# Loads of a residual input issued ahead, and LayerNorm sums with the data as the moving operand

## The chip, the cores and the metric

The kernel runs on one core of a Trainium2 chip. A core has a matrix engine (TensorE, PE in the profile, with its weight loads PEld), a vector engine (VectorE, DVE), an activation engine (ScalarE, ACT), a programmable vector engine (GpSimd, POOL) and an engine that here only issues transfers (SyncE, SP). Each engine works off its own instructions in order and waits on semaphores for the others. PE reads its operands from SBUF, 128 partitions wide, and writes to PSUM. In a matmul the stationary operand is loaded first and the moving operand then streams through it. POOL and SP each have a queue of DMA transfers. The metric is the device time of one execution in microseconds.

## What is computed

One layer of a hybrid decoder on 256 prompt tokens and 8 x 4 sample tokens (N = 288), model width 2048:

```python
mod = silu(c) @ w_ada + b_ada
sh1, sc1, g1, sh2, sc2, g2 = split(mod, 6)
u = layernorm(x) * (1 + sc1) + sh1
p = u @ w_in                       # gated short convolution | mLSTM heads | output gate o
...
mix = concat(y_conv, y_mlstm) @ w_out
x = layernorm(ALPHA * x + (1 + g1) * mix) * ln1_g + ln1_b
u2 = layernorm(x) * (1 + sc2) + sh2
a, g = split(u2 @ w_up, 2)
y = (silu(causal_dwconv3(a)) * g) @ w_down
x = layernorm(ALPHA * x + (1 + g2) * y) * ln2_g + ln2_b
```

All values are float32; the states of convolution and mLSTM are further outputs. The change lies at the first residual: the loading of `x` for `ALPHA * x`, and the sums over the 2048 features that the two layer norms behind it need.

## The kernel before

Activations lie with features on the partitions and tokens along the free dimension: a tile is 128 features x 288 tokens, and x is 16 tiles. Weights come in 128 x 128 blocks, 16 to a transfer of 1 MB (`raw`), in the order of a list `items` that `plan()` makes; SP issues the transfers as far as seven buffers allow. Each half of a transfer is split into a high part (`whi`, ACT, L314) and a low part (`wlo`, DVE, L327), two halves ahead of use, and each block is multiplied three times (`mm3`, L474 to L476). Other items of the list hold 1 MB of `w_ada` (kind `"a"`); `take()` runs such an item on PE at once (L381: eight instructions `adaps`), and `next_block()` takes those that stand ahead of the next weight block.

Stages around the change, in the program's order: the columns of the convolution (`hc`, `cg`, `bg`), the eight columns of the output gate (`o`), the 16 tiles of the output projection (`mix`, loop over m), then the first up columns (`up`).

Ahead of the o columns stands the loop that loads x again on POOL's queue, 144 KB a tile, into `xa` and scales it on POOL by ALPHA (L1081, L1082). Each mix tile m ends in `residual(xa[m], ...)` (L1234 to L1238, DVE: `xa += g1 * mix`, the 32 sample tokens apart). Behind tile 0 the side work `first_stats` has PE average tile 0 over its features (L1302), ACT copies the result out as `shift` (L1304), POOL subtracts it from `xa[1]` and `xa[2]` (L1306) and, called by `stats(m)`, from each further tile (L1296), and DVE from `xa[0]` (L1308). `stats(m)` then takes, per tile, three weighted accumulations (L1266, L1268) and three plain ones (L1275, L1278) on DVE, two squares on ACT (L1282, L1283). The last tile is not accumulated.

In the last mix tile and behind it, `sums` (L1368) has PE add over the features. The six columns are the mean z, three weighted sums w, x, b, the square q and the weighted square p. The data block of 128 tokens is the stationary operand and a column of 1/2048 the moving one, so that tokens come out on the partitions: three matmuls a sum, which PE runs as six instructions. The last tile's four linear sums come from one matmul with `w4` (four columns). From the result `S` a chain of small DVE and ACT instructions (L1423 to L1455, on 128 x 3 values in `sv`) makes both norms' scales; `tokens` (L1460) turns them back to feature layout (`rr`, copied to `R`, and `tokp`, copied to `tok`). `corr` (L1500) and `u2t` (L1493 to L1504) then make the operand of the up columns.

The last adaLN unit (g2, 16 items) is taken in parts: `G2_EARLY` items stand in the list ahead of the first up column (one is taken by `take()` among the sums, `G2_FIRST` ahead of `rr`, what is left behind `u2_hi(0)`), the others are mixed into the up columns.

Of the kernel before, what the change touches and what calls it, by code (L numbers as in the profile page):

```python
# [7 lines left out]
F32 = mybir.dt.float32  # L8
F32R = mybir.dt.float32r
AF = mybir.ActivationFunctionType  # L10
ALU = mybir.AluOpType

P = 128
# [4 lines left out]
N = NP + NS  # L18
# [15 lines left out]
LATE = 15  # L34
KOUT = 6
PREHI = 3
G2_FIRST = 2
CF_AT = 6
SUMS_AT = 11
UP_AT = 12  # L40
# [1 line left out]
STORES = [(0,), (1, 2), (3, 4, 5), (6, 7, 8), (9, 10, 11), (12, 13, 14), (15,)]  # L42
RES0 = 8
RES1 = 12
G2_EARLY = 5
MIX_LAST = 8
C_FIRST = 2
C_LAST = 3
# [165 lines left out]
def body(tc, d, off, items, blocks):  # L214
    nc = tc.nc
    V, A, G, T = nc.vector, nc.scalar, nc.gpsimd, nc.tensor
    from contextlib import ExitStack
    ctx = ExitStack()
    with ctx:
        pers = ctx.enter_context(tc.tile_pool(name="pers", bufs=1))  # L220
# [15 lines left out]
        def st(name, dt=F32):  # L236
            return slab.tile([P, N], dt, tag="t", name=nm(name))

        def mps(name, n=512):
            return misc.tile([P, n], F32, tag="m", name=nm(name))  # L240
# [20 lines left out]
        for i, a in enumerate(range(0, KB, 3)):  # L261
            b = min(a + 3, KB)
# [4 lines left out]
        pos = [0, 0]  # L267
# [9 lines left out]
        c = 0  # L277
# [84 lines left out]
        ones = pers.tile([P, P], F32, name="ones")  # L362
        badd = pers.tile([P, 6, KB], F32, name="badd")
        ident = sm("ident")
# [71 lines left out]
        def take():  # L436

            i = pos[0]
            it = items[i]
            load()  # L440
            r = raws.pop(i)
            pos[0] += 1
            if it[0] == "a":
                ada_item(it, r)
                free()
            else:
                c_item(it[1], r)
# [109 lines left out]
        for k in range(0, KB, 2):  # L557
            t = st("xsum")
# [9 lines left out]
        for k in range(KB):  # L568
            x, q = st("xc"), st("sq")
# [35 lines left out]
        S = {}  # L605
# [15 lines left out]
        stat = pers.tile([P, 6], F32, name="stat")  # L621
# [456 lines left out]
        xa = []  # L1078
        for m in range(KB):
            t = st("xa")  # L1080
            nc.gpsimd.dma_start(out=t, in_=xd[:, m])  # L1081
            G.tensor_scalar(t, t, ALPHA, None, ALU.mult)  # L1082
            xa.append(t)
        gb = pers.tile([P, 8, KB], F32, name="gb")
        bb1, gg, gbb, ngg2, gbb2, gs, ng = (gb[:, i] for i in range(7))
        w4 = pers.tile([P, 4], F32, name="w4")
        L = KB - 1
        tmp3 = pers.tile([P, 3, 8], F32, name="gbt3")
        cst = pers.tile([P, 6], F32, name="cst")
# [2 lines left out]
        def constants_1():  # L1092
            ps = mps("gbm", 2)
            T.matmul(ps, ones, tmp[:, :, 0], start=True, stop=True)
            yield 2
            V.tensor_copy(gbm, ps)

            yield 6
            V.tensor_scalar(bb1, b1v, gbm[:, 1:2], None, ALU.subtract)
            V.tensor_tensor(gg, g1v, g1v, ALU.mult)  # L1100
            V.tensor_tensor(gbb, g1v, bb1, ALU.mult)
            V.tensor_scalar(ngg2, gg, -2.0, None, ALU.mult)
            V.tensor_scalar(gbb2, gbb, 2.0, None, ALU.mult)
            V.tensor_scalar(ng, g1v, -1.0, None, ALU.mult)
            V.tensor_copy(w4[:, 0:1], ones[:, 0:1])
            for i, v in enumerate((g1v, ngg2, gbb2)):
                V.tensor_scalar(w4[:, i + 1:i + 2], v[:, L:L + 1], ones[:, 0:1], None, ALU.mult)
            V.tensor_tensor(gb[:, 7], bb1, bb1, ALU.mult)
            for j, v in enumerate((gg, gbb2, gb[:, 7])):
                V.tensor_tensor(tmp3[:, j, 0:8], v[:, 0:8], v[:, 8:16], ALU.add)  # L1110
                for n in (4, 2, 1):
                    V.tensor_tensor(tmp3[:, j, 0:n], tmp3[:, j, 0:n], tmp3[:, j, n:2 * n], ALU.add)
            yield 10
            ps = mps("gbm3", 3)
            T.matmul(ps, ones, tmp3[:, :, 0], start=True, stop=True)
            yield 2
            V.tensor_copy(cst[:, 0:3], ps)
            V.tensor_scalar(cst[:, 3:4], gbm[:, 0:1], -1.0, None, ALU.mult)
            V.tensor_scalar(cst[:, 4:5], cst[:, 1:2], -1.0, None, ALU.mult)
            V.tensor_scalar(cst[:, 5:6], cst[:, 2:3], EPS, None, ALU.add)  # L1120
# [125 lines left out]
        BLK = ((0, P), (P, 2 * P), (N - P, N))  # L1246
# [110 lines left out]
        stp = {}  # L1357

        def sums(name, x, c, stop=False):

            bank = c // 5
            start = bank not in stp
            if start:
                stp[bank] = mps("stat", 24)
            w = 4 if name == "lin" else 1
            rhs = w4 if name == "lin" else ones[:, 0:1]
            for i, (a, b) in enumerate(BLK):
                T.matmul(stp[bank][:, 8 * i + c:8 * i + c + w], x[:, a:b], rhs, start=start and i == 0,  # L1368
                         stop=stop and i == 2)

        def late_sums():
            yield SUMS_AT
# [38 lines left out]
        q, p = squares(KB - 1)  # L1411
        sums("z", acc1["z"], 0)
        sums("q", acc1["q"], 4)
        take()
        sums("lin", xa[KB - 1], 0)
        sums("q", q, 4, True)
        sums("p", p, 5, True)
        S, S5 = (stp[i].rearrange("p (b c) -> p b c", c=8) for i in range(2))
        c = [sv[:, :, i] for i in range(16)]
        mean, wp, wv, xv, bv, var1, t1, t2, r1, v2, r2, Rr = c[0:12]  # L1420
        MW = sv[:, :, 0:2]
# [10 lines left out]
        V.tensor_tensor(xv, xv, mean, ALU.mult)  # L1432
        for _ in s1:
            pass
        V.tensor_tensor(xv, xv, S5[:, :, 5], ALU.add)
        V.tensor_tensor(t1, wp, wp, ALU.mult)
        V.tensor_tensor(xv, xv, t1, ALU.subtract)
        V.tensor_tensor(xv, xv, r1, ALU.mult)
# [23 lines left out]
        def spread(j):  # L1462
            return lambda i: sv[:, i, j:j + 1].to_broadcast([P, P])

        for _ in range(G2_FIRST):
            if items[pos[0]][0] == "a":
                take()
        rps = mps("rr", N)
        tokens(rps, spread(11), P)
        R = st("R")  # L1470
# [69 lines left out]
        for j in (8, 12):  # L1540
            ps = mps("rb", N)
            tokens(ps, spread(j), P)
            t = st("rb")
# [237 lines left out]
```

## Time and profile before

| | us |
|---|---|
| median of 3 runs | 1559.61 |
| lowest and highest run | 1556.93, 1560.07 |
| profiled execution | 1565.79 |
| its span, first to last instruction | 1564.0 |
| PE busy | 1515.3 |
| DVE, ACT, POOL busy | 948.0, 588.4, 251.9 |

The mean granted clock of the profiled execution is 0.984. The profile is of one execution; its rows name engine, source line, operation and `out<-in` tiles, with start and duration in us, and in brackets the idle time of the engine before it and what ended it. A row of the table by stretches of time gives busy us of PE, PEld, DVE, ACT and POOL, the granted TensorE clock as a share of full speed, the DMA engines' share and GB/s. A float32 matmul of the program appears as two PE instructions. A PE that is called busy isn't always streaming: the profile counts an instruction's time whatever its size.

### The profile page before, as it was taken

The numbers are of one execution on the slowest core, as the hardware profiler recorded it, in microseconds if no ns is written. First come the engines' busy times: TensorE is split into PE (matmuls) and PEld (weight loads), VectorE is DVE, ScalarE is ACT, GpSimd is POOL, SyncE is SP. The second block draws the span as 40 slices with busy tenths as digits, with TensorE's granted clock in tenths as the row PEclk, the third lists the DMA queues.
The fourth block names the chain that finished last, engine by engine and source line by source line (L and its number), as shares of the span: only waits on it lengthen the run. The fifth ranks groups of instructions, "written<-read, shape, count | busy, mean of one in ns | idle before, by whom it ended". The sixth has DMA issues, their size and how long they took to land.

```text
span 1564.0 us, 28234 instructions
## 1 busy us (share of the span) xinstructions
PE 1515.3 (97%) x11762; PEld 1418.0 (91%) x11762; DVE 948.0 (61%) x1746; ACT 588.4 (38%) x880; POOL 251.9 (16%) x472
## 2 busy tenths in 40 slices
PE   9999999999999969999999999999999999999994
PEld 7988988888888859979999999999999999999994
DVE  6466566777865388677655545555555545555557
ACT  5533243422233224444433333344443334444334
POOL 3310005210112320003740000000000000000245
PEclk9999999999999979889999999999999999999997
DMA  9897778668898845364755644444444444444401
GB/s 387 342 346 297 285 301 324 236 225 341 326 372 316 299 173 208 135 243 145 259 204 228 222 162 165 161 170 173 168 166 166 162 164 170 173 167 165 162 28 61
DMA packets 49663, 343.90 MB, mean 220 GB/s; under 512 B 5888, under 2 KB 6400, under 8 KB 9088
## 3 DMA queue, kind: packets, MB, share of 16 engines
q1 hardware_dynamic: 46656, 329.09, 56.8%
q0 software_dynamic: 2736, 12.82, 2.1%
q8 instruction: 92, 1.51, 0.4%
q14 instruction: 35, 0.29, 0.1%
q10 hardware_dynamic: 144, 0.19, 0.0%
HBM read 329.77 MB, written 12.31 MB: 219 GB/s over the span
## 4 chain that ended last, share of the span: by engine, by line
PE 85%; DVE 5%; DMA 3%; issue 3%; POOL 2%; ACT 1%; SPq 0%; POOLq 0%; DVEq 0%; ACTq 0%
PE g L474 6%; PE g L476 5%; PE a L474 5%; PE g L475 5%; PE dn L476 5%; PE dn L474 5%; PE dn L475 5%; PE a L476 5%; PE a L475 5%; PE adaps L381 5%; PE h L474 5%; PE h L475 4%; PE h L476 4%; DMA xa<-xT 2%; PE mix L474 2%
## 5 line engine op out<-in xcount | busy, mean ns | idle before, releaser
L314 ACT CAST whi<-raw 128x1024 fp32r<-128x1024 f32 x410 | 424.1, 1046 | 402.8 <-PE dn L476 156.6
L327 DVE TENSOR_TENSOR wlo<-raw,whi 128x1024 fp32r<-128x1024 f32 x410 | 502.3, 1240 | 55.4 <-ACT whi L314 54.6
L476 PE MATMUL dn<-y2h,whi 128*128 128x288 f32 x704 | 208.0, 295 | 0.0
L474 PE MATMUL dn<-y2l,whi 128*128 128x288 f32 x704 | 207.7, 295 | 0.0
L475 PE MATMUL dn<-y2h,wlo 128*128 128x288 f32 x704 | 207.5, 295 | 0.0
L475 PE MATMUL a<-u2h,wlo 128*128 128x288 f32 x656 | 193.5, 295 | 1.3 <-DVE wlo L327 1.3
L474 PE MATMUL a<-u2l,whi 128*128 128x288 f32 x656 | 194.4, 296 | 0.0
L474 PE MATMUL g<-u2l,whi 128*128 128x288 f32 x656 | 194.3, 296 | 0.0
L476 PE MATMUL g<-u2h,whi 128*128 128x288 f32 x656 | 193.5, 295 | 0.0
L476 PE MATMUL a<-u2h,whi 128*128 128x288 f32 x656 | 193.5, 295 | 0.0
L475 PE MATMUL g<-u2h,wlo 128*128 128x288 f32 x656 | 193.2, 295 | 0.0
L474 PE MATMUL h<-ul,whi 128*128 128x288 f32 x512 | 155.8, 304 | 2.8 <-DVE hp L1004 1.5
L475 PE MATMUL h<-uh,wlo 128*128 128x288 f32 x512 | 151.6, 296 | 0.0
L476 PE MATMUL h<-uh,whi 128*128 128x288 f32 x512 | 151.2, 295 | 0.0
L474 PEld LDWEIGHTS dn<-y2l,whi 128*128 128x128 f32 x704 | 132.3, 188 | 0.1
L475 PEld LDWEIGHTS dn<-y2h,wlo 128*128 128x128 f32 x704 | 132.3, 188 | 0.1
L476 PEld LDWEIGHTS dn<-y2h,whi 128*128 128x128 f32 x704 | 132.2, 188 | 0.0
L1043 POOL COPY fnew<-hal 128x2 f32<-128x2 f32 x44 | 8.9, 203 | 744.3 <-ACT hal L1575 744.3
L474 PEld LDWEIGHTS a<-u2l,whi 128*128 128x128 f32 x656 | 123.2, 188 | 5.0 <-issue 4.2
L474 PEld LDWEIGHTS g<-u2l,whi 128*128 128x128 f32 x656 | 123.2, 188 | 4.2 <-ACT hal L1576 3.4
L475 PEld LDWEIGHTS a<-u2h,wlo 128*128 128x128 f32 x656 | 123.2, 188 | 1.7 <-DVE wlo L327 1.7
L475 PEld LDWEIGHTS g<-u2h,wlo 128*128 128x128 f32 x656 | 123.2, 188 | 0.0
(453 smaller groups left out, 2928.0 us busy)
## 6 DMA issues: line engine op xcount, KB each, us to landing
raw<-wst SPq DMA_DIRECT2D x300, 1024.0 KB, 4.9
raw<-cst SPq DMA_DIRECT2D x8, 1024.0 KB, 5.3
cs_o<-raw POOLq DMA_DIRECT2D x8, 1024.0 KB, 10.9
xa<-xT POOLq DMA_DIRECT2D x16, 144.0 KB, 4.9
xin<-xT SPq DMA_DIRECT2D x5, 432.0 KB, 5.6
y_o<-yout SPq DMA_DIRECT2D x4, 432.0 KB, 2.5
cp_o<-cnew POOLq DMA_DIRECT2D x8, 128.5 KB, 7.2
raw<-wst SPq DMA_DIRECT2D x2, 512.0 KB, 14.0
```

The lines of the kernel that those rows point to most:

```text
L314: A.copy(his[n], raws[i][:, hf * 1024:(hf + 1) * 1024])
L327: V.tensor_tensor(lo, r, hi.bitcast(F32), ALU.subtract)
L381: T.matmul(ps[32 * s:32 * s + 32, 0:n], csil[:, k, :], r[:, c0:c0 + n], start=(k == 0), stop=(k == 15))
L474: T.matmul(ps, hi, ul, start=start, stop=False)
L475: T.matmul(ps, lo, uh, start=False, stop=False)
L476: T.matmul(ps, hi, uh, start=False, stop=stop)
L1043: G.tensor_copy(dst[:, 0, :], hal[:, NP:NP + 2])
```

## The change

Three things change. The 16 loads of x are issued in a row, and the 16 scalings follow in a loop of their own. The sums are formed the other way around: an operand of eight columns is stationary (`pick8[:, c]` with one column of 1/2048 and seven of zero, or `w8` for the last tile) and the whole tile of 288 tokens moves, so all nine sums accumulate into one PSUM tile of 8 x 288; ACT copies that to SBUF (`rows`), and three matmuls against a piece of the identity turn it to tokens on partitions. And of the 16 g2 items, six instead of five stand ahead of the up columns, four of them taken right behind the turns and none among the sums.

```diff
-G2_FIRST = 2
+G2_FIRST = 4
-G2_EARLY = 5
+G2_EARLY = 6
...
             nc.gpsimd.dma_start(out=t, in_=xd[:, m])
+            xa.append(t)
+        for t in xa:
             G.tensor_scalar(t, t, ALPHA, None, ALU.mult)
-            xa.append(t)
...
-        w4 = pers.tile([P, 4], F32, name="w4")
+        w8 = pers.tile([P, 8], F32, name="w8")
+        pick8 = pers.tile([P, 6, 8], F32, name="pick8")
...
-            V.tensor_copy(w4[:, 0:1], ones[:, 0:1])
+            V.memset(w8, 0.0)
+            V.memset(pick8, 0.0)
+            for i in range(6):
+                V.tensor_copy(pick8[:, i, i:i + 1], ones[:, 0:1])
+            V.tensor_copy(w8[:, 0:1], ones[:, 0:1])
...
         def sums(name, x, c, stop=False):
 
-            bank = c // 5
-            start = bank not in stp
+            start = not stp
             if start:
-                stp[bank] = mps("stat", 24)
-            w = 4 if name == "lin" else 1
-            rhs = w4 if name == "lin" else ones[:, 0:1]
-            for i, (a, b) in enumerate(BLK):
-                T.matmul(stp[bank][:, 8 * i + c:8 * i + c + w], x[:, a:b], rhs, start=start and i == 0,
-                         stop=stop and i == 2)
+                stp[0] = mps("stat", N)
+            T.matmul(stp[0][0:8], w8 if name == "lin" else pick8[:, c], x, start=start, stop=stop)
...
         sums("z", acc1["z"], 0)
         sums("q", acc1["q"], 4)
-        take()
         sums("lin", xa[KB - 1], 0)
-        sums("q", q, 4, True)
+        sums("q", q, 4)
         sums("p", p, 5, True)
-        S, S5 = (stp[i].rearrange("p (b c) -> p b c", c=8) for i in range(2))
+        rows = st("rows")
+        A.copy(rows[0:8], stp[0][0:8])
+        S = mps("statc", 24)
+        for i, (a, b) in enumerate(BLK):
+            T.matmul(S[:, 8 * i:8 * i + 8], rows[0:8, a:b], ident[0:8, 0:8], start=True, stop=True)
+        S = S.rearrange("p (b c) -> p b c", c=8)
+        for _ in range(G2_FIRST):
+            if items[pos[0]][0] == "a":
+                take()
...
-        V.tensor_tensor(xv, xv, S5[:, :, 5], ALU.add)
+        V.tensor_tensor(xv, xv, S[:, :, 5], ALU.add)
...
-        for _ in range(G2_FIRST):
-            if items[pos[0]][0] == "a":
-                take()
         rps = mps("rr", N)
```

What POOL holds at the start of the loads, before (`xa` with a number is one tile of x, `cnew` the convolution's new state):

```order
L1075 DMA conv_o<-cnew_3575 128x144
L1081 DMA xa_5401<-xT 128x288
L1082 TENSOR_SCALAR xa_5401<-xa_5401 128x288
L1081 DMA xa_5404<-xT 128x288
L1082 TENSOR_SCALAR xa_5404<-xa_5404 128x288
L1081 DMA xa_5407<-xT 128x288
L1082 TENSOR_SCALAR xa_5407<-xa_5407 128x288
```

And now, the last two loads, the first and last scalings, and what follows them on POOL:

```order
L1081 DMA xa_5429<-xT 128x288
L1081 DMA xa_5431<-xT 128x288
L1084 TENSOR_SCALAR xa_5401<-xa_5401 128x288
...
L1084 TENSOR_SCALAR xa_5431<-xa_5431 128x288
L1256 DMA tok_1036_6103<-tok 128x288
L1258 MEMSET tt_6105 128x288
L1312 TENSOR_TENSOR xa_5403<-xa_5403,shift_1051_6203 128x288
L1312 TENSOR_TENSOR xa_5405<-xa_5405,shift_1051_6203 128x288
```

No scaling stands between two loads any more; the subtractions of the shift stay behind all of them.

On PE, from the last mix matmul to the matmuls that turn the scales back (`rr`), before (`raw` of `adaps` is a piece of w_ada, `az`, `ln1q`, `ln1p` the accumulated sums or the last tile's squares):

```order
L476 MATMUL mix_7352<-yh_6089,whi_7291 128x288
L1368 MATMUL stat_7383<-ones,az_6270 128x1 x3
L1368 MATMUL stat_7383<-ones,ln1q_6207 128x1 x3
L381 MATMUL adaps_7431<-raw_6805,csil 32x512 x4
L1368 MATMUL stat_7383<-w_5450,xa_5446 128x4 x3
L1368 MATMUL stat_7383<-ones,ln1q_7421 128x1 x3
L1368 MATMUL stat_7393<-ones,ln1p_7422 128x1 x3
L381 MATMUL adaps_7431<-raw_6879,csil 32x512 x4
L381 MATMUL adaps_7431<-raw_7046,csil 32x512 x4
L1460 MATMUL rr_7492<-small,sv 128x128 x2
```

and now:

```order
L476 MATMUL mix_7361<-yh_6098,whi_7300 128x288
L1370 MATMUL stat_7392<-az_6279,pick_5451 8x288
L1370 MATMUL stat_7392<-ln1q_6216,pick_5451 8x288
L1370 MATMUL stat_7392<-xa_5431,w_5450 8x288
L1370 MATMUL stat_7392<-ln1q_7421,pick_5451 8x288
L1370 MATMUL stat_7392<-ln1p_7422,pick_5451 8x288
L1422 MATMUL statc_7432<-small,rows_7430 128x8 x3
L381 MATMUL adaps_7436<-raw_6814,csil 32x512 x4
L381 MATMUL adaps_7436<-raw_6888,csil 32x512 x4
L381 MATMUL adaps_7436<-raw_7055,csil 32x512 x4
L381 MATMUL adaps_7436<-raw_7133,csil 32x512 x4
L1468 MATMUL rr_7494<-small,sv 128x128 x2
```

Three matmuls a sum have become one, the item among the sums has moved behind them, and the three turns (`statc`) with four items now stand between the sums and `rr`.

More of the change, by code (lines that the diff above doesn't have):

```diff
@@ L1104, in constants_1 @@
             V.tensor_scalar(ng, g1v, -1.0, None, ALU.mult)
-            V.tensor_copy(w4[:, 0:1], ones[:, 0:1])
+            V.memset(w8, 0.0)
[3 more added lines that the diff above has]
+            V.tensor_copy(w8[:, 0:1], ones[:, 0:1])
             for i, v in enumerate((g1v, ngg2, gbb2)):
-                V.tensor_scalar(w4[:, i + 1:i + 2], v[:, L:L + 1], ones[:, 0:1], None, ALU.mult)
+                V.tensor_scalar(w8[:, i + 1:i + 2], v[:, L:L + 1], ones[:, 0:1], None, ALU.mult)
             V.tensor_tensor(gb[:, 7], bb1, bb1, ALU.mult)
```

## Prediction

> **What bounds the kernel now.** I read the page first.
>
> ```profile
> span 1564.0 us, 28234 instructions
> PE 1515.3 (97%) x11762; PEld 1418.0 (91%) x11762; DVE 948.0 (61%) x1746; ACT 588.4 (38%) x880; POOL 251.9 (16%) x472
> PEclk9999999999999979889999999999999999999997
> ```
>
> PE is the bound nearly throughout, so time is to be had only where PE stands still, does extra work, or runs at a lower clock. PEclk dips in two places (slices 15, 17 and 18, about 550 and 660 us), and the change touches both. Next the table by windows (length; busy us of PE, PEld, DVE, ACT, POOL; granted clock; DMA share; GB/s):
>
> ```profile
> 547.00:550.40 3.40, 0.00 (x0) 0.00 (x0) 3.10 (x3) 0.00 (x0) 3.40 (x6) 1.00 0.07 24
> 550.40:553.80 3.40, 0.00 (x0) 0.00 (x0) 3.40 (x1) 0.00 (x0) 3.40 (x5) 0.50 0.00 0
> 564.00:567.40 3.40, 3.40 (x16) 3.40 (x16) 3.40 (x7) 1.14 (x2) 0.00 (x0) 0.50 0.90 364
> 567.40:570.80 3.40, 3.40 (x28) 3.14 (x31) 0.70 (x2) 1.05 (x1) 0.00 (x0) 0.99 0.99 366
> 601.60:605.00 3.40, 2.38 (x18) 1.83 (x14) 3.33 (x11) 1.81 (x3) 0.00 (x0) 1.00 0.96 357
> 652.80:656.20 3.40, 3.40 (x32) 3.40 (x30) 1.92 (x4) 0.00 (x0) 0.00 (x0) 1.00 0.28 113
> 656.20:659.60 3.40, 3.40 (x16) 3.40 (x16) 0.00 (x0) 0.00 (x0) 0.00 (x0) 0.50 0.00 0
> ```
>
> The clock is 0.50 from 550.4 to 567.4 and again from 656.2. The first fall follows an idle PE. The second follows a window in which PE is called busy but mostly runs one-column matmuls.
>
> **First place.** The waits of PE and of DVE (520 to 600 us), then POOL in order of time:
>
> ```profile
> PE mix L475 <- DVE wlo L327: 14.5, 1, 14.5
> DVE xa L1234 <- POOL xa L1306: 11.7, 1, 11.7
> 450.49 0.56 POOL L1081 DMA_DIRECT2D xa<-xT  x1
> 457.09 0.95 POOL L1082 TENSOR_SCALAR xa<-xa 128x288 f32<-128x288 f32 x1 [6.04 <-DMA xa<-xT]
> 544.64 0.92 POOL L1082 TENSOR_SCALAR xa<-xa 128x288 f32<-128x288 f32 x1 [1.97 <-DMA xa<-xT]
> 546.42 1.56 POOL L1306 TENSOR_TENSOR xa<-xa,shift 128x288 f32<-128x288 f32 x2
> 547.93 9.76 POOL L1296 TENSOR_TENSOR xa<-xa,shift 128x288 f32<-128x288 f32 x13
> ```
>
> POOL issues one load of x, waits for its landing, scales it, issues the next: 16 round trips from 450.5 to 545.6, of which the first and last scaling are shown. The subtractions of the shift queue behind them. DVE and PE, same stretch:
>
> ```profile
> 532.52 0.41 ACT L1304 ACTIVATE shift<-shift 128x288 f32<-128x288 f32 x1 [3.26 <-PE shift L1302]
> 534.30 1.22 DVE L327 TENSOR_TENSOR wlo<-raw,whi 128x1024 fp32r<-128x1024 f32 x1
> 547.88 9.86 DVE L1238 TENSOR_TENSOR xa<-xa,rs 128x32 f32<-128x32 f32 x1
> 546.55 0.40 PE L474 MATMUL mix<-yl,whi 128*128 128x288 f32 x1
> 561.45 0.61 PE L475 MATMUL mix<-yh,wlo 128*128 128x288 f32 x1 [14.50 <-DVE wlo L327]
> 578.30 0.48 DVE L1234 SCALAR_TENSOR_TENSOR xa<-mix,mod,xa 128x256 f32<-128x256 f32 x1 [1.98 <-PE mix L476]
> 585.88 0.48 DVE L1234 SCALAR_TENSOR_TENSOR xa<-mix,mod,xa 128x256 f32<-128x256 f32 x1 [1.98 <-PE mix L476]
> ```
>
> The shift is ready at 532.9. POOL takes it at 546.4, DVE then stands 9.86 us in a 32-column addition while POOL runs 13 subtractions, and the next weights (wlo) reach PE at 561.4.
>
> **The change, part by part.**
>
> *Loads of x.* The scaling over its 16 instructions (min, median, max ns):
>
> ```profile
> L1082 POOL TENSOR_SCALAR xa<-xa x16: 920/924/1788, 457.1 to 544.6; 128x288 f32<-128x288 f32 x16
> ```
>
> An issue costs POOL 0.56 us and a scaling 0.92 (median). With all issues ahead, the first eight go out as their buffers come free; eight semaphores take turns, so the ninth waits for the first landing (6.0 us after issue). Some issues also wait for a PE or ACT instruction that released the buffer. All of these stand earlier in the program than the o columns, so before about 459. That puts the last issue at 462 to 467, the last landing by 475, and 16 x 0.92 = 14.7 us of scaling ends at 477 to 490. The shift at 532.9 then finds POOL idle, and the 14.5 us wait goes.
>
> The slow restart goes with it. A mix tile at full clock takes 7.58 us (585.88 less 578.30): 48 matmuls and one adaLN item,
>
> ```profile
> 743.51 1.06 PE L381 MATMUL adaps<-raw,csil 128*32 128x512 f32 x8
> ```
>
> so (7.58 - 1.06)/48 = 0.136 a matmul. At half clock 18 of them take 4.46 (below), 0.248 each. From 561.45 to 567.45 PE lost 6.0 x (1 - 0.136/0.248) = 2.7. Sum **17.2**.
>
> What the loads now collide with: 16 x 0.147 = 2.4 MB come within some 20 us instead of 95, beside the weights.
>
> ```profile
> 445.00:460.00 15.00, 14.14 (x107) 11.21 (x106) 9.71 (x24) 4.43 (x5) 2.95 (x6) 1.00 1.02 422
> 455.64 1.06 ACT L314 CAST whi<-raw 128x1024 fp32r<-128x1024 f32 x1 [3.19 <-DMA raw<-wst]
> 467.78 0.40 PE L474 MATMUL o<-ul,whi 128*128 128x288 f32 x1
> ```
>
> The transfers are full there (1.02). 2.4 MB at 422 GB/s delays weights by up to 5.6 us. The weights cast at 455.64 are those that PE multiplies from 467.78, 12 us later, so I cost the delay at nothing; without that cover it is 5.6.
>
> *POOL beside DVE.* From 532.9 POOL runs 15 subtractions on end (11.3 us by 9.76/13 each) while DVE works off tile 0, a split, tile 1 and its six statistics. The nearest rows on sharing:
>
> ```profile
> 1515.40 4.31 POOL L1165 TENSOR_TENSOR xa<-xa,ln2shift 128x288 f32<-128x288 f32 x5 [1.33 <-ACT ln2shift L1163]
> 1515.43 2.07 DVE L1151 TENSOR_TENSOR xa<-xa,ln2shift 128x288 f32<-128x288 f32 x2 [2.00 <-ACT ln2shift L1163]
> ```
>
> Released by the same ACT instruction, as here, the two alternate: DVE takes 1.04 us each and POOL 0.86 (4.31/5), where alone it takes 0.75 (9.76/13). Up to the split that PE wants at 546.7 DVE has fifteen instructions, two splits of 1.2 and the rest 0.2 to 1.04: done at 545 to 547.5, a stall of 0 to 0.8. If the row of 9.86 repeats, DVE stands until the burst ends (some 545.6, as the first five alternate) and delivers 3.7 later, as before (557.74 to 561.45): 549.3, a stall of 2.6. I take **0.5**, near the alternating rows, which are released alike. The Trainium skill (SBUF — State Buffer, section Who interferes with whom) says that a DVE instruction with two SBUF inputs and a GpSimd instruction reading SBUF block each other for one whole instruction. By that rule the term is 0; the 9.86 us beside thirteen instructions of 0.75 is far more than the rule allows.
>
> *Feature sums.* PE before, the first copy of the sums on DVE, and the end of the first chain:
>
> ```profile
> 653.97 0.72 PE L1368 MATMUL stat<-ones,aw 128*128 128x1 f32 x6
> 656.92 0.59 PE L474 MATMUL mix<-yl,whi 128*128 128x288 f32 x1
> 661.38 1.27 PE L1368 MATMUL stat<-ones,az 128*128 128x1 f32 x6
> 662.31 0.19 DVE L1238 TENSOR_TENSOR xa<-xa,rs 128x32 f32<-128x32 f32 x1
> 668.49 0.16 DVE L1423 COPY sv<-stat 128x3 f32<-128x3 f32 x1 [5.99 <-PE stat L1368]
> 672.44 0.17 DVE L1450 TENSOR_TENSOR sv<-sv 128x3 f32<-128x3 f32 x1
> 673.23 0.85 PE L1460 MATMUL rr<-small,sv 128*128 128x128 f32 x6
> 531.83 0.65 PE L1302 MATMUL shift<-xa,ones 128*128 128x288 f32 x2
> 532.45 0.29 PE L475 MATMUL mix<-yh,wlo 128*128 128x288 f32 x1
> ```
>
> A sum was six instructions; now it is two that move 288 columns. The shift's pair (531.83 to 532.45, less one mix matmul of 0.13) prices it at 0.49. An eight-column stationary isn't in the trace: bounds are 0.24 (half) and 0.98 (four passes); I take 0.49, since matmuls here go by moving columns.
> - Four sums inside the last tile: 2.95 (653.97 to 656.92) becomes 1.95: -1.0.
> - If the clock holds, the 18 mix matmuls after them take 18 x 0.136 = 2.45 instead of 4.46: -2.0.
> - From E, the last mix matmul, to the rr matmuls: 11.85 before (661.38 to 673.23). Now the last tile is ready at E + 1.1 (662.50), three sums 1.5, their end 0.2, the copy to SBUF 0.4 (the shift's copy takes 0.41), three turns 0.8 (like aw's six, 0.72), DVE's chain 4.1 (668.49 to 672.61) and a start of 0.2: 8.3 to 8.4: -3.4. The added copy and turns, 1.2, lie on this path and are in it.
> - tokp waits for DVE a little longer behind rr, since rr no longer comes late: +0.2.
>
> *adaLN items of G2.* One of them costs PE 1.0 to 1.06. Before, one stood among the sums and two ahead of rr; now four stand behind the turns, 4.0 us under DVE's chain of 4.1. Two remain before the first up tile, as before. So one fewer stands in the dense part: -1.0. Eight small DVE instructions to fill the new stationary operands lie in the o columns, where DVE is below half busy: nothing.
>
> Second place: 1.0 + 2.0 + 3.4 - 0.2 + 1.0 = **7.2**. In all 17.2 + 7.2 - 0.5 = **23.9**.
>
> The profiled execution took 1565.8 (span 1564.0 and 1.8 around it); with the change 1541.9. The median of the runs is 6.2 lower, 1559.6. No row says where the 6.2 lies, so I take the same gain off the median: **1535.7**.
>
> **Rivals.**
>
> *Eight-column sums don't hold the clock.* For it: the window from 652.8 fell though PE was called busy. Against it: there one column moved, here 288, and the window at 601.6 kept its clock with 2.38 of 3.40 busy. Price: the four items take 7.1 us (669.66 to 673.23 for two, before) and end later than the chain, leaving 0.3 of the 3.4; two more items and the start of up at half clock cost 2.5. The second place gives 1.0 + 2.0 + 0.3 - 2.5 + 1.0 = 1.8, the total 18.5, the time 1541.1. The Trainium skill (TensorE: Matmul & The Clock Gate, section Why this matters for your kernels) asks only that PE have no idle gap over some 3 us. By that rule the clock would not have fallen at 656.2, where it did.
>
> *The burst of subtractions blocks DVE* as the row of 9.86 shows: 2.6 of stall and 0 to 2.7 for a slow restart, 4.0 in the middle instead of 0.5: 1539.2.
>
> *The profile's 6.2 us lie in the round trips,* which would then be quicker without it: gain 17.7, time 1541.9. For it: they are the one long serial stretch off PE. Against it: nothing shows them slowed.
>
> *Slower: POOL's bursts shut DVE out until they end.* Scaling at the longest row of before, 1.79 us, lasts 28.6 from about 463 to 492. The next split after 463 is wanted an o column (some 8 us) behind 467.78 and would come at 493: 17 of stall and 2.7 for the restart. The second burst of 11.3, shut likewise from 532.9, ends at 544.2; the splits behind it come 5 and 1.5 late, and 2.7 for the restart. 29 against a gain of 24.4 gives 1564. It decides from 24.4 on. Against it: the alternating rows, and that POOL, not DVE, waited in the long scalings.
>
> **How the numbers follow.** Forecast 0.52 (its own range 1531 to 1539, from a sum's price of 0.24 or 0.98, nine of them, and the stall of 0 or 2.6); clock not held 0.16; DVE blocked 0.17; profile's excess 0.10; slower 0.03; two of these together, near 1545, 0.02. The range 1530.5 to 1543 holds the first four but for their tails. A measurement of this kernel tells about 0.2%, 3 us, from no change. Faster 0.95, same 0.02, slower 0.03.
>
> **What would show it.** Right: the 16 issues of xa within some 17 us from 450.5, no wait of PE on wlo near 547, PEclk at 9 in all slices but the last, sums of two instructions at 0.24 us apart, rr about 8.4 us behind the last mix matmul, ten G2 items among the up tiles. Wrong: a half clock after the sums, a DVE addition of several us around 538, PE waiting for raw near 460 to 480, or xa issues still spread out.

## The result and the profile after

| | before | after |
|---|---|---|
| median of 4 runs, us | 1558.27 | 1543.23 |
| lowest and highest run | 1554.15, 1560.07 | 1541.22, 1544.06 |
| profiled execution, and its span | 1565.79, 1564.0 | 1543.43, 1541.6 |

The four runs of before are the three given above and one more (1554.15). The ratio is 0.9905 (95% interval 0.9882 to 0.9929): 15.0 us faster where 23.9 were forecast, and 0.2 above the range. Between the two profiled executions, though, the gain is 22.4. So the sum was nearly right for the execution it was read from, and wrong for the median.

The page of the changed kernel, then two of PE's waits between 440 and 700 us, and the table by windows for two stretches (length; busy us of PE, PEld, DVE, ACT, POOL; clock; DMA share; GB/s):

```profile
span 1541.6 us, 28186 instructions
PE 1506.6 (98%) x11732; PEld 1408.7 (91%) x11732; DVE 945.0 (61%) x1754; ACT 588.7 (38%) x881; POOL 258.0 (17%) x472
PEclk9999999999999999999999999999999999999997
```

```profile
PE stat L1370 <- DVE ln1p L1284: 1.1, 1, 1.1
PE rr L1468 <- DVE sv L1458: 0.7, 1, 0.7
```

```profile
545.00:565.00 20.00, 20.00 (x149) 16.82 (x148) 18.30 (x34) 7.44 (x11) 5.36 (x4) 1.00 0.75 285
640.00:680.00 40.00, 36.37 (x260) 28.79 (x261) 31.12 (x97) 16.25 (x29) 0.00 (x0) 1.00 0.62 240
```

PE has no wait on `wlo` near 547 any more, both dips of the clock are gone, and a small wait on `ln1p` is new. POOL in order of time (start, duration), the first and last issue of x among them:

```profile
452.20 3.78 POOL L1081 DMA_DIRECT2D xa<-xT  x7
...
468.46 0.55 POOL L1081 DMA_DIRECT2D xa<-xT  x1 [1.52 <-PE o L476]
469.03 17.77 POOL L1084 TENSOR_SCALAR xa<-xa 128x288 f32<-128x288 f32 x16
...
534.19 1.85 POOL L1312 TENSOR_TENSOR xa<-xa,shift 128x288 f32<-128x288 f32 x2 [24.24 <-ACT shift L1310]
536.00 14.36 POOL L1302 TENSOR_TENSOR xa<-xa,shift 128x288 f32<-128x288 f32 x13
```

The 16 issues take 16.8 us, the scalings end at 486.8, and the shift finds POOL idle for 24.24 us. DVE beside POOL's subtractions, and PE from the last mix matmul to `rr`:

```profile
539.87 0.39 DVE L1244 TENSOR_TENSOR xa<-xa,rs 128x32 f32<-128x32 f32 x1
540.29 0.99 DVE L1274 SCALAR_TENSOR_TENSOR aw<-xa,small,aw 128x288 f32<-128x288 f32 x1
```

```profile
643.62 0.29 PE L476 MATMUL mix<-yh,whi 128*128 128x288 f32 x1
643.85 0.65 PE L1370 MATMUL stat<-az,pick 128*8 128x288 f32 x2
644.33 0.65 PE L1370 MATMUL stat<-ln1q,pick 128*8 128x288 f32 x2
...
652.20 0.82 PE L1468 MATMUL rr<-small,sv 128*128 128x128 f32 x6 [0.73 <-DVE sv L1458]
```

The addition that stood 9.86 us takes 0.39. POOL's 13 subtractions take 1.10 each instead of 0.75 and DVE's accumulations 0.99 instead of 0.52: the two engines take turns. A sum costs 0.48, and `rr` comes 8.6 us behind the last mix matmul.

### The profile page after: what moved, and what is told of

The parts are those of the page before. It is cut to its first block, busy times and chain, and to the rows that moved or that the text cites. A ratio compares the mean times of both kernels' runs of the same rounds, so it can differ in the third digit from the quotient of the medians.

```text
span 1541.6 us, 28186 instructions
## 1 busy us (share of the span) xinstructions
PE 1506.6 (98%) x11732; PEld 1408.7 (91%) x11732; DVE 945.0 (61%) x1754; ACT 588.7 (38%) x881; POOL 258.0 (17%) x472
## 4 chain that ended last, share of the span: by engine, by line
PE 90%; DVE 5%; ACT 1%; DMA 1%; issue 1%; POOL 0%; SPq 0%; DVEq 0%; ACTq 0%; POOLq 0%
PE g L474 6%; PE g L476 6%; PE g L475 5%; PE a L474 5%; PE a L476 5%; PE dn L476 5%; PE dn L475 5%; PE a L475 5%; PE dn L474 5%; PE adaps L381 5%; PE h L474 5%; PE h L475 4%; PE h L476 4%; PE mix L474 2%; PE mix L475 2%; PE mix L476 2%
## 5 line engine op out<-in xcount | busy, mean ns | idle before, releaser
L476 PEld LDWEIGHTS g<-u2h,whi 128*128 128x128 f32 x656 | 123.4, 188 | 0.0
## 6 DMA issues: line engine op xcount, KB each, us to landing
cs_o<-raw POOLq DMA_DIRECT2D x8, 1024.0 KB, 11.2
xa<-xT POOLq DMA_DIRECT2D x16, 144.0 KB, 10.1
```

Of the source, the lines that this page charges most:

```text
L476: T.matmul(ps, hi, uh, start=False, stop=stop)
```

## Experiments

The stages below are worked out from the starts of matmuls in the traces (us, each figure rounded by itself). They begin at the first mix matmul, 63.6 to 63.9 us behind the first o matmul in every run; what lies ahead of that differs by up to 3.9 us between executions and isn't part of the change. E is the last mix matmul, U the first up matmul. The clock column gives the stretches at half clock between 640 and 680 us.

| profile | PE's wait on wlo | first mix to E | E to rr | rr to U | U to end | sum | half clock |
|---|---|---|---|---|---|---|---|
| before | 14.5 | 137.8 | 12.1 | 4.4 | 886.4 | 1040.6 | 17.1 |
| before_a | 8.2 | 129.1 | 8.6 | 5.4 | 886.4 | 1029.5 | 6.8 |
| before_b | 11.2 | 131.3 | 8.3 | 6.6 | 886.4 | 1032.5 | 6.8 |
| before_c | 10.8 | 131.4 | 9.0 | 5.0 | 886.4 | 1031.7 | 6.8 |
| sums_only | 12.3 | 132.9 | 8.6 | 4.5 | 884.6 | 1030.5 | none |
| loads_only | none | 118.3 | 8.3 | 6.6 | 886.7 | 1019.8 | 6.8 |
| loads_only_2 | none | 119.7 | 9.1 | 5.0 | 886.7 | 1020.5 | 3.4 + 6.8 |
| after | none | 119.1 | 8.6 | 4.5 | 884.9 | 1017.1 | none |
| after_2 | none | 119.1 | 8.6 | 6.2 | 884.8 | 1018.7 | 3.4 |

### The kernel before, profiled again

> The kernel before, unchanged, profiled again. Its profiled execution of 1565.8 us was slower than each of its four counted runs (1554.2 to 1560.1), and the forecast took a gain read from that one execution off the median. Theory A: the 9.86 us in which DVE stood in a 32-column addition is a matter of chance; in a usual execution DVE alternates with POOL there, so PE's wait on wlo is 6 to 9 us instead of 14.5, and the execution takes 1555 to 1560. Theory B: the sixteen round trips are quicker in a usual execution; then the last scaling ends ahead of 545.6 by as much as the wait is shorter (below 540 for a wait of 8), and the addition still takes several us. Theory C: the stall is the same in each execution (14.5, last scaling at 545 to 546, addition of 9.9 us), and the 7.5 us lie elsewhere, in slow-clock stretches or waits that come and go.

> The kernel before once more, to see whether the stall of one execution is that of the next. Theory A: wait on wlo and the length of DVE's addition go together and vary between executions (addition 0.2 to 10 us, wait 6 to 14.5) with the last scaling at 545 to 546 each time. Theory B: the end of the last scaling varies by several us. Theory C: all three within 1 us of the first profile.

> The kernel before, unchanged, a fourth profile. By the rule found so far: DVE's addition 9.8 to 10 us; PE's wait on wlo is the end of the last scaling less the first mix matmul less 7.65, somewhere from 8 to 15; the slow clock at the sums lasts 6.8 us where it sets in behind the last mix matmul and 14 to 17 where it sets in ahead of it, with rr then 12 us behind that matmul instead of 8.2 to 9.1.

They took 1554.07, 1558.46 and 1558.09 us. PE's waits, POOL's last scaling and DVE's addition, of before_a, then of before_b, then PE's wait of before_c:

```profile
PE mix L475 <- DVE wlo L327: 8.2, 1, 8.2
537.46 0.92 POOL L1082 TENSOR_SCALAR xa<-xa 128x288 f32<-128x288 f32 x1 [4.80 <-DMA xa<-xT]
540.70 9.96 DVE L1238 TENSOR_TENSOR xa<-xa,rs 128x32 f32<-128x32 f32 x1
```

```profile
PE mix L475 <- DVE wlo L327: 11.2, 1, 11.2
541.93 0.92 POOL L1082 TENSOR_SCALAR xa<-xa 128x288 f32<-128x288 f32 x1 [2.35 <-DMA xa<-xT]
545.18 9.90 DVE L1238 TENSOR_TENSOR xa<-xa,rs 128x32 f32<-128x32 f32 x1
```

```profile
PE mix L475 <- DVE wlo L327: 10.8, 1, 10.8
```

Theory B holds for the wait. The addition is as long each time (9.86 to 9.96), so theory A falls. What varies is the round trips: POOL's 16 waits for a landing add up to 68.2 us in the first profile and to 61.6, 64.5 and 64.2 in the others. With the end of the last scaling counted from the first mix matmul (22.2, 15.7, 18.8 and 18.4 us), PE's wait is that less 7.6 to 7.7 each time: a microsecond of round trips is a microsecond of PE. Theory C, that the excess lies in slow-clock stretches, holds for the rest. The table by windows from 640 to 680 us, of the first profile, of before_a and of before_c:

```profile
640.00:680.00 40.00, 39.52 (x252) 33.16 (x251) 21.70 (x71) 11.15 (x22) 0.00 (x0) 0.79 0.48 172
```

```profile
640.00:680.00 40.00, 38.32 (x273) 32.27 (x272) 27.59 (x85) 13.06 (x23) 0.00 (x0) 0.91 0.58 211
```

```profile
640.00:680.00 40.00, 38.28 (x273) 32.28 (x273) 26.94 (x86) 14.10 (x25) 0.00 (x0) 0.91 0.59 223
```

The half clock at the sums lasted 17.1 us (a mean of 0.79 over 40) in the profile that the forecast used and 6.8 in the three others. In that profile it had begun 4.9 us ahead of E, so that the sums ran in it, and E to rr took 12.1. In before_a and before_c it began 4.0 and 3.5 behind E, where PE waits for DVE's chain anyway, and in before_b 9.8 behind E, so behind `rr`, where it shows as 6.6 instead of 4.5 from rr to U. The first profile's sum is 9.4 above the mean of the three others (1031.3). It was a slow draw, not a faulty one: of 64 counted runs of before over all comparisons, two took longer than its 1565.79 us. A variant of before shown further down, swap_parts, drew the like (1566.24 us: a wait of 14.7, and 12.1 from E to rr with 13.7 us at half clock from 1.7 ahead of E).

### One part alone

loads_only is the diff's new loop of loads without the rest of the change; sums_only is the rest of the change with the old loop.

> The kernel before with the 16 loads of x issued in a row and scaled in a loop of their own; sums, turns and g2 items as before. If my steps hold in every execution (17.2 less 0.5): 16.7 below before, about 1541.6 against a median of 1558.3, and the second place would then have been worth nothing. If the typical stall is smaller than the profiled one (theories A and B): the second place's 7.2 stands, and the first gives 15.0 - 7.2 = 7.8, so about 1550.5. In its profile PE has no wait on wlo near 547, and the half clock behind the sums (from about 640) is still there.

> The changed kernel with the loads of x in turn with their scalings again; eight-column sums, turns and the placing of g2 items as in the changed kernel. If the second place is worth 7.2 as forecast: 1551 against 1558.3, with rr about 8.4 us behind the last mix matmul and no slow clock there. If the first place were worth its full 16.7 in usual executions: 1558 to 1560, no gain. The stall of PE on wlo near 547 is still there, of whatever length it has in this execution.

loads_only: 1545.47 against 1556.3, ratio 0.9921 (0.9892 to 0.9951). sums_only: 1556.13, ratio 0.999 (0.9968 to 1.0011). The 7.2 us of the second place aren't seen; the interval allows -1.7 to 5.0. The changed kernel and loads_only were then measured again:

> The changed kernel again, in more rounds, beside the kernel with the loads ahead alone. What the two differ by is the second place (sums, turns, g2 items). Forecast step: 7.2 us. Theory from the new profiles of before: the slow clock at the sums lasted 17.1 us in the profile that I used and 6.8 in the two others, where rr came 8.3 to 8.6 us behind the last mix matmul and not 12.1; then the second place is worth 3.0 us (from the first o matmul to the end 1080.7 against 1083.7). So this kernel at about 1543 and the other at 1546 by the theory, at 1550 by the forecast step.

> The kernel before with only the loads of x ahead, again in more rounds. Theory (second place 3.0): 3 us slower than the changed kernel, about 1546. Forecast step (7.2): 7 slower, 1550. In its profile no wait of PE on wlo near 547, and one slow-clock stretch of 6.8 us (or of 10 to 17, by chance) around the sums.

after_2: 1543.25 (0.9909, 0.9889 to 0.9930). loads_only_2: 1546.08 (0.9925, 0.9908 to 0.9941). By these medians the second place is worth 2.8 us, though the runs of the two kernels overlap (1541.55 to 1548.0 and 1544.03 to 1547.26); by the stages it is 2.2. The loads alone measured 10.8 and 11.3.

The table shows what the second place is made of. From loads_only to after, the first stage grows by 0.8 and E to rr by 0.3; rr to U shrinks by 2.1, since no half clock lies there, and U to the end by 1.8. So the sums, as placed here, lose about a microsecond, and what pays lies behind them. The old sums with the moved g2 items alone were not run, so how much the turned-around sums have to do with the kept clock isn't shown.

### What DVE stands for

> The kernel before (loads in turn with scalings, old sums), but the 13 subtractions of the shift from tiles 3 to 15 run on DVE, each in its tile, so that POOL has no burst behind tile 1. Every profile of the serial loads so far has one addition of 9.9 us on DVE beside that burst, whatever the length of the round trips. Theory: POOL's burst holds DVE up; the addition then takes 0.2 us, and PE's wait on wlo is 9.9 us shorter than (end of the last scaling less first mix matmul less 7.65), so 0 to 4.6 us; the time 1546 to 1549 against 1556.3, though DVE gets 13 x 0.46 = 6 us more to do in tiles that leave it 2 us each. Rival: the addition waits for something else of POOL (a buffer, the end of the round trips); then it still takes several us and the time is that of before or worse by up to 6.

```diff
             if 0 < m < KB - 2:
-                G.tensor_tensor(xa[m + 2], xa[m + 2], shift1[0], ALU.subtract)
+                V.tensor_tensor(xa[m + 2], xa[m + 2], shift1[0], ALU.subtract)
```

PE's wait and the addition in its trace:

```profile
PE mix L475 <- DVE wlo L327: 4.6, 1, 4.6
547.50 0.19 DVE L1238 TENSOR_TENSOR xa<-xa,rs 128x32 f32<-128x32 f32 x1
```

1548.86 us, ratio 0.9942 (0.9922 to 0.9962). The last scaling ended 21.6 us behind the first mix matmul. By the rule above (21.6 less 7.65) the wait would have been 13.9 with the burst of subtractions on POOL; without it, it is 4.6. So some 9 us of PE's wait was the burst, and only what is left was lateness of the loads alone. Why the same addition takes its turn in the changed kernel was tried in five kernels:

> The changed kernel, but POOL also subtracts the shift from tile 0, so that DVE's first statistics are released by a POOL instruction while POOL runs on with 15 subtractions, as in the kernel before, where DVE stood 9.9 us. In the changed kernel DVE and POOL were released by the same ACT instruction and took turns. Theory: who is first decides; DVE is shut out until POOL's 16 subtractions of 0.75 end, at about 12 us behind the shift, no instruction of POOL is longer than 0.8, a DVE instruction takes some 8 to 11 us, and PE waits 1 to 4 us on wlo near 549: 1544 to 1549. Rival: turns are taken whoever is first, and the lock of before has another cause (its short 32-column addition behind an instruction that reads PSUM); then POOL's subtractions take about 1.1 each, no DVE instruction is over 2 us, and the time is that of the changed kernel within 1 us.

```diff
-            for m in (1, 2):
+            for m in (0, 1, 2):
                 G.tensor_tensor(xa[m], xa[m], sh, ALU.subtract)
             yield 2
-            V.tensor_tensor(xa[0], xa[0], sh, ALU.subtract)
```

> The kernel before (loads in turn, old sums) with the two parts of the residual swapped: DVE does the 32 sample columns of a tile (two short instructions) ahead of the 256 prompt columns. What is open is why DVE stands 9.9 us beside POOL's 13 subtractions here and takes turns with them in the changed kernel. Theory: the first DVE instruction with two SBUF operands that meets a running burst is shut out until the burst ends, whatever its size; then the 32-column addition, now 0.4 us earlier beside the first subtractions, stands 10 us or more. Rival: the instant matters, or the short addition behind an instruction that reads PSUM; then it takes its turn (0.2 to 1 us), the lock falls on another instruction or on none, and in the last case PE's wait on wlo is 5 to 9 us shorter than the end of the last scaling less the first mix matmul less 7.65.

> The kernel pool_first (POOL subtracts the shift from tile 0 too) with one more DVE instruction ahead of the first statistics, released by POOL's first subtraction: a two-operand subtraction over 128 x 288 into a scratch tile that nothing reads. In pool_first the first DVE instruction beside the burst was a scaling with one SBUF operand and took its turn. Theory 1, the first two-operand DVE instruction that meets a burst already running is shut out until its end: this instruction takes about 11 to 12 us. Theory 2, only a short one (32 columns) is: this one takes 0.5 to 1.3 us. Theory 3, the lock belongs to the serial loads or to what ran ahead of the burst: 0.5 to 1.3 us.

> As first_wide, but the added instruction is over the 32 sample columns alone (128 x 32), like the addition that stood 9.9 us. Theories 1 and 2: it takes 11 to 12 us. Theory 3: 0.2 to 1 us.

> The kernel before (loads in turn, old sums) with one DVE scaling (one SBUF operand, 128 x 288, into a scratch tile that nothing reads) ahead of tile 1's residual, so that the first DVE instruction beside POOL's burst is the kind that took its turn. Theories 1 and 2: if the first meeting decides, DVE and POOL then take turns, the addition takes 0.2 to 1 us, and PE's wait on wlo is 4 to 8 us shorter than the end of the last scaling less the first mix matmul less 7.65. If each short or two-operand instruction is at risk anew, the addition still stands about 9 us and the wait is as long as by that rule, plus up to 0.9.

swap_parts, in `residual`; then the line added in first_wide, in first_short (both to pool_first, ahead of `stats(0)`) and in first_scalar (to the kernel before, ahead of tile 1's `residual`):

```diff
-            V.scalar_tensor_tensor(dst[:, 0:NP], ps[:, 0:NP], mod[:, g, m, 0:1], dst[:, 0:NP],
-                                   ALU.mult, ALU.add)
             t = halop.tile([P, NB, TS], F32, tag="rs", name=nm("rs"))
             V.tensor_tensor(t, smp(ps), bc_t(mod[:, g, m, 1:9]), ALU.mult)
             V.tensor_tensor(smp(dst), smp(dst), t, ALU.add)
+            V.scalar_tensor_tensor(dst[:, 0:NP], ps[:, 0:NP], mod[:, g, m, 0:1], dst[:, 0:NP],
+                                   ALU.mult, ALU.add)
...
+            V.tensor_tensor(scr, xa[0], sh, ALU.subtract)
...
+            V.tensor_tensor(scr[:, NP:N], xa[0][:, NP:N], sh[:, NP:N], ALU.subtract)
...
+                V.tensor_scalar(scr, xa[1], 1.0, None, ALU.mult)
```

pool_first took 1541.88 us (4 runs); swap_parts, first_wide, first_short and first_scalar, of one run each, took 1566.24, 1543.03, 1542.74 and 1556.01. The DVE instructions in question, in the order above; for pool_first the first one beside the burst, and the addition:

```profile
534.09 0.90 DVE L1272 TENSOR_SCALAR aw<-xa,small 128x288 f32<-128x288 f32 x1 [1.80 <-POOL xa L1312]
538.99 0.19 DVE L1244 TENSOR_TENSOR xa<-xa,rs 128x32 f32<-128x32 f32 x1
```

```profile
549.65 10.48 DVE L1236 TENSOR_TENSOR xa<-xa,rs 128x32 f32<-128x32 f32 x1 [8.75 <-POOL xa L1306]
```

```profile
534.01 1.05 DVE L1315 TENSOR_TENSOR scr<-xa,shift 128x288 f32<-128x288 f32 x1 [1.80 <-POOL xa L1313]
```

```profile
533.96 0.78 DVE L1315 TENSOR_TENSOR scr<-xa,shift 128x32 f32<-128x32 f32 x1 [1.80 <-POOL xa L1313]
```

```profile
542.08 10.70 DVE L1396 TENSOR_SCALAR scr<-xa 128x288 f32<-128x288 f32 x1 [5.52 <-POOL xa L1307]
```

Neither the engine that is first nor the size or kind of DVE's instruction decides: that is theory 3. In all seven profiles in which POOL came to the full burst straight from the serial loads, the first DVE instruction with operands in SBUF alone that met the running burst was shut out to its end; in all in which POOL had stood idle for some 24 us ahead of it, the two took turns. What in this makes the difference stays open. Two things that go with it weren't separated: the transfer issue and the memset on POOL just ahead of the burst, and DVE's own idle time ahead of it (5.3 to 11.8 us in the seven profiles, 0.9 to 1.8 in the others). A standstill of PE or of the transfers didn't set it off: in before_a PE was busy for all of the 3 us from 540.0, in which the lock began, and the transfers had a share of 0.83.

### What the second place is worth, and two better versions

> The changed kernel with none of the six early g2 items behind the turns (all six stand where two stand now, ahead of the second corr matmul). Step of the forecast: four items lie under DVE's chain and cost nothing; without them PE stands about 4 us idle there and does the items later, 3.6 to 4.0 us more, and 1547. Theory of the clock: the items, not the eight-column sums alone, keep PE streaming between the sums and up; without them a window of 3.4 us is nearly empty and the clock falls, for 2 to 3 us more: 1548 to 1550, with a slow-clock stretch of 6.8 us or so near 650 in the profile. Rival: the sums hold the clock by themselves and the items cost the same wherever they stand: 1543 to 1544, no slow clock.

```diff
-G2_FIRST = 4
+G2_FIRST = 0
```

```profile
PE rr L1468 <- DVE sv L1458: 4.3, 1, 4.3
640.00:680.00 40.00, 33.18 (x215) 24.30 (x216) 24.82 (x80) 12.92 (x23) 0.00 (x0) 0.87 0.53 212
```

1548.74 us, 5.5 above the changed kernel: PE stands 4.3 us under DVE's chain, and the clock falls for 10.2 us. So the eight-column sums don't hold the clock by themselves; with the four items behind the turns it mostly holds, and the items lie there at no cost.

> The changed kernel with the four late sums two blocks of 16 later in the last mix tile (SUMS_AT 13 instead of 11). In the changed kernel the fourth of them waits 1.1 us for DVE's last accumulation, so that the stretch from the first to the last of the four takes 3.35 us where the old six-instruction sums take 2.6; this is the one place where the new sums lose. Theory: the wait goes and nothing takes its place: last mix matmul 1.1 to 1.4 us earlier behind the first mix tile (119.1 us from the first to the last mix matmul becomes 117.7 to 118.0), 1542 against 1543.2, too little for the times and seen in the profile alone. Rival: the later sums collide with the wait of PE for something else of the last tile (the split ahead of up, at block 12): no gain.

> Three small edits to the changed kernel: late sums two blocks later (worth 1.1 to 1.4 by the wait on DVE's last accumulation), POOL subtracts the shift from tile 0 too (0.5 of DVE off the start of the statistics, no wait of PE there, so 0 to 0.5), and a fifth g2 item behind the turns, seven early in all (one item of 1.0 us leaves the dense up columns, 0.7 of it fits into the wait of rr on DVE's chain: 0.7 to 1.4). Sum 1.8 to 3.3: about 1540.5 against 1543.2. Rival: a seventh early item takes a transfer buffer from the first up weights, PE waits for weights at the start of up, and the time is that of the changed kernel or 1 to 5 us above it.

> The changed kernel with five early g2 items as before instead of six (four behind the turns, one ahead of up, eleven among the up columns). In the changed kernel ACT stands 7.9 us on a weights transfer in the last mix tiles, the squares of tile 14 queue behind that cast, DVE's last accumulation behind them, and PE's fourth late sum waits 1.1 us; with old sums and five items that transfer had landed and ACT did not wait. Theory: the sixth early item takes one of the seven transfer buffers and so delays the weights; with five the wait of PE on the last accumulation goes (from first to last mix matmul 118.0 instead of 119.1), and the eleventh item among the up columns costs 1.0 to 1.7 behind them; in sum 1543 to 1544. Rival: the new sums, being quicker, only come too early for DVE; then the 1.1 us stay, and the time is 1544 to 1545.

sums_late (`SUMS_AT = 13`) took 1541.13 us (0.9893, 0.9854 to 0.9932). From the first mix matmul to E it takes 118.4, so 0.7 of the 1.1 was gained. better (`SUMS_AT = 13`, `G2_EARLY = 7`, `G2_FIRST = 5` and the edit of pool_first) took 1542.63; its rival came true, with PE waiting ahead of up:

```profile
PE up L474 <- ACT whi L314: 2.0, 1, 2.0
PE up L475 <- DVE wlo L327: 0.9, 1, 0.9
```

g2_old (`G2_EARLY = 5`) took 1542.49 (0.9895, 0.9864 to 0.9926), with 117.8 from the first mix matmul to E and 885.9 from U to the end: the item among the up columns costs 1.0 behind U, and 1.3 come back ahead of E. The cause is seen on ACT in the last mix tiles, first of the changed kernel, then of g2_old:

```profile
638.32 1.04 ACT L314 CAST whi<-raw 128x1024 fp32r<-128x1024 f32 x1 [7.89 <-DMA raw<-wst]
639.27 0.44 ACT L1288 ACTIVATE ln1q<-xa 128x288 f32<-128x288 f32 x1
```

```profile
630.86 1.05 ACT L314 CAST whi<-raw 128x1024 fp32r<-128x1024 f32 x1 [0.86 <-DMA raw<-wst]
634.54 0.45 ACT L1288 ACTIVATE ln1q<-xa 128x288 f32<-128x288 f32 x1 [2.63 <-DVE xa L1244]
```

With a sixth early item the weights for up land late, ACT's cast waits for them, tile 14's squares queue behind the cast, DVE's accumulation behind these, and the fourth sum on PE behind that. The same wait of ACT is 7.8 to 8.1 us in sums_only, g2_none, sums_late and best, which have six items, and 0.8 in before_a and loads_only, which have five. Whether the item does it by holding one of the seven buffers, or by its own 1 MB ahead of the weights in the queue, isn't shown.

> The changed kernel with the late sums two blocks later (this alone measured 1541.1) and POOL subtracting the shift from tile 0 too (alone 1541.9), without the seventh early g2 item that cost a wait on weights. Theory: 0.7 of the wait on the last accumulation and 0 to 0.5 of DVE: 1540 to 1541.5 against 1543.2 of the changed kernel. Rival: the two medians near 1541 came from executions without a slow-clock stretch, by chance, and this one gives 1542 to 1543.

best (`SUMS_AT = 13` and the edit of pool_first) took 1540.82, ratio 0.988 (0.9855 to 0.9906), the lowest median. It is 2.4 below the changed kernel, whose runs (1541.55 to 1548.0) overlap with its own (1539.45 to 1543.05). Its profiled execution had a half clock of 3.4 us and was the slowest of its six runs (1543.05), so that profile can't exclude the rival. The granted clock of each run speaks against it: at 0.995 best took 1539.91 and the changed kernel 1541.22 to 1541.90, at 0.994 1539.45 and 1540.79 against 1543.03 to 1543.43. The stages show 1.2 of the 2.4, and the later sums alone give that (sum 1015.9 in sums_late, 1017.1 in after). The edit of pool_first shows nothing there that is clear of the differences between executions (1016.9).

## Why the prediction was wrong

**The step that failed** is the last of the sum: "No row says where the 6.2 lies, so I take the same gain off the median". The table of times did say that something was unusual: the profiled execution stood above all counted runs. Its excess lay in the two terms that the change takes away, so off the median they were worth less. The rival "the profile's 6.2 us lie in the round trips" (0.10, 1541.9) came nearest, and named about half of the cause: of the 9.4 by which that profile exceeds the three others, 4.4 is PE's wait (14.5 against a mean of 10.1), and nearly all of the rest is where the slow clock at the sums fell. Against this rival stood "nothing shows them slowed". One execution can't show that. That the 16 waits ran from 1.97 to 6.04 us in that single trace was a sign that their sum could vary.

For the execution that it was read from the sum came out well: its stages from the first mix matmul to the end are 23.5 us longer than those of after. From the mean of the three other profiles of before to the two of the changed kernel it is 13.3, near the 15.0 and 14.1 measured between medians.

Stage by stage, in the profile's own terms:

- First place, 17.2 less 0.5: right for that execution. With the last tile's 3.0 the forecast from the first mix matmul to E was 19.7, and 18.6 was measured. PE's wait and the half clock behind it are gone; the issues (16.8 us, "within some 17"), the end of the scalings (486.8, "477 to 490"), the collision with the weights (nothing: PE has no wait on weights there) and DVE and POOL taking turns came as forecast. Between medians, 10.8 and 11.3 of the 16.7 were measured. In the three other profiles of before the wait is 8 to 11 us, which makes this term some 4 too large; sums_only, swap_parts and first_scalar, with the same loads and burst, waited 12.3, 14.7 and 9.4. The reading was also incomplete: the wait took both the late loads and the burst.
- "Four sums inside the last tile: -1.0": wrong in sign. Old sums at full clock take 2.6, not 2.95, and the new ones 3.3, with the wait on `ln1p`. Where that wait is gone (g2_old) they take 2.0.
- "18 mix matmuls at full clock: -2.0" and "E to rr: 11.85 to 8.4": the after side is right (8.6 from E, 8.4 from the first sum behind E, where the 11.85 began). The before side hung on when the clock fell. In the three other profiles E to rr is 8.3 to 9.0, so the 3.4 were -0.3 to 0.4, and the 2.0 were nothing where the fall comes behind E.
- "adaLN items: -1.0": 1.5 to 1.9 behind U. One item is 1.0 of it (g2_old); the rest was not followed up.
- The second place in all: 7.2 forecast, 2.8 measured between medians, 2.2 between the profiles' mean sums.
- "Eight-column sums don't hold the clock" (0.16): g2_none shows that they don't by themselves. With the items behind the turns the fall came in three of the ten profiles with new sums (after_2, better, best), behind `rr`, for 3.4 us, and cost 1.7 in after_2 (rr to U 6.2 instead of 4.5). "The burst blocks DVE" (0.17) did not come, and neither did the slower rival.

The slow stretches came in lengths of 3.4, 6.8, 10.2, 13.7 and 17.1 us, and their start stood differently to E in each execution. The Trainium skill (TensorE: Matmul & The Clock Gate, section What's actually happening) says that activity is watched in a free-running window of 3413 ns; the lengths agree, as all are multiples of it. What a thin stretch of PE costs is therefore partly chance (E to rr took 8.3 to 12.1 in four executions of one program), and one profile gives one draw.

## What to carry to other kernels

Compare the profiled execution's own time with the runs before any gain is read off it. If it is above them, ask which of the terms that you sum could vary from one execution to the next (chains of transfer round trips, stretches at low clock), and price these below what that trace shows. Further profiles of the unchanged kernel show how far they vary; here three did.

A serial chain that ends just behind the point where PE needs it costs its variation in full, and taking it off the path also narrows the runs: ten runs of sums_only, with the loads in turn, took 1551.1 to 1560.6, and ten of g2_none, with the loads ahead, 1547.2 to 1549.7. Filler work has its price in the queues that it occupies: a sixth early item saved 1.0 behind U and cost 1.3 ahead of E.

## What was not expected of the hardware

- A DVE instruction can be shut out by a whole run of POOL instructions, not only by one: 9.9 us beside 13 subtractions of 0.75 in five profiles, 10.5 for the same addition in swap_parts and 10.7 for a scaling with a single SBUF operand in first_scalar, so in each of the seven profiles with the serial loads and the burst. The Trainium skill (SBUF — State Buffer, section Who interferes with whom) says that the one that issues first has the shared port pair for its whole instruction, and the other is blocked meanwhile; the turns in the changed kernel (1.0 each) agree with that, these rows don't.
- The landing of a 144 KB load beside the weights stream varied: POOL's 16 waits for one, 1.97 to 6.04 us each, added up to 61.6 to 68.2 us in four executions of the same program.
